# Start addresses of SBUF tiles in a two-layer encoder trunk, moved to multiples of 512 bytes

## Chip, core and metric

The kernel runs on one core of a Trainium2 chip. The metric is device time in microseconds (us) of one execution. A core has five engines with queues of their own: PE (TensorE, matrix products; its weight loads are shown apart as PEld), DVE (VectorE), ACT (ScalarE), POOL (GpSimd) and SP (SyncE, which here only issues DMA transfers). SBUF is the on-chip memory of 128 partitions that they work from; a tile is a range of bytes, the same in every partition. PSUM holds the results of PE.

## What is computed

Two layers of an encoder for one sequence of 512 tokens with 1024 features, everything in float32. Layer 0 mixes tokens with a state-space scan, layer 1 with a gated MLP; each is followed by a gated convolutional channel mixer, and every sub-layer by a layer norm.

```
for i in range(2):
    y = mamba2_mixer(x, ...) if i == 0 else spatial_gating_mixer(x, ...)
    x = layer_norm(DN_ALPHA * x + y, ln_g[i, 0], ln_b[i, 0])
    f = conv_ffn(x, ffn_w_in[i], ffn_conv_w[i], ffn_conv_b[i], ffn_w_out[i])
    x = layer_norm(DN_ALPHA * x + f, ln_g[i, 1], ln_b[i, 1])

def mamba2_mixer(x, ...):
    z, xbc, dt = split(x @ w_in)                 # 1024 -> 6176
    xbc = silu(causal_dwconv(xbc, conv_w, conv_b))
    y = ssd_scan(...) + d_skip * xs              # chunked state-space scan
    return rms_norm(y * silu(z), norm_g) @ w_out # 2048 -> 1024

def spatial_gating_mixer(x, ...):
    u, v = split(gelu(x @ w_in + b_in))          # 1024 -> 2 x 2048
    v = layer_norm(v, ln_g, ln_b)
    v = einsum('gts,bnsgc->bntgc', tril(w_s), v) + b_s
    return (u * v) @ w_out                       # 2048 -> 1024

def conv_ffn(x, ...):
    g, u = split(causal_dwconv(x @ w_in, conv_w, conv_b))  # 1024 -> 2 x 2816
    return (silu(g) * u) @ w_out                 # 2816 -> 1024
```

## The kernel before

Every large product is made from three PE products in the type float32r. Each operand is split into a rounded part `hi` and a rest `lo`, and `hi*hi + hi*lo + lo*hi` is added up in PSUM. All weights lie in one DRAM tensor of 244 pieces of 128 x 1024. `w_prep` brings each of them in: SP issues the load of `wraw` (3 buffers), ACT rounds it to `whi`, DVE subtracts to get `wlo` (7 buffers each), up to six pieces ahead of their use.

A matmul has a stationary operand, loaded into the array by a LDWEIGHTS of 128 columns of 4 bytes, and a moving operand that is streamed through it, here mostly 512 columns (2048 bytes in each partition). In this kernel every matmul has a weight load of its own. There are three kinds of products:

- Input projections (`mm_k`, lines 121 to 123, results `ip`): the weights `whi`/`wlo` are stationary, the activations `xT_hi`/`xT_lo` are moving. Eight of the tiles are done in two halves of 256 tokens (`InProj.pre` and `post`), so that PE has work while a layer norm ends.
- Output projections (`out_proj`, lines 211 to 213, results `acc`): the activations `ahi`/`alo` are stationary, the weights are moving. There are four: after the state-space scan (W_SO, 16 steps), after the first channel mixer (W_F1O, 22), after the gated MLP (W_GO, 16) and after the second channel mixer (W_F2O, 22).
- The v half of the gated MLP (`v_tile`, lines 560 to 562, results `pv`): `xT_hi`/`xT_lo` are stationary, the weights are moving. The first four tiles are started by `v_start`, while the layer norm before them ends; line 604 then adds the bias `bvb`, which ACT's queue loads at line 599 in four pieces (2 buffers).

What stands between them (scan, transposes, spatial product) uses plain float32 matmuls.

Tiles come from pools. `const` and `wpool` are laid out first and stay for the whole kernel; the other pools are opened and closed with the stages and take the space above, so a tile of one stage can lie on bytes that tiles of the stage before held, and its first writer then waits for their last reader. The allocator places every tile at the next multiple of 32 bytes. The order of each engine's instructions comes from a scheduler that follows the program's order and the waits. Some tiles are small: `nhalf` (16 numbers in a partition, the exponent of the reciprocal root on POOL), `ea`, `nsl`, `cd`, `rv` in the scan, and `st`, `mv`, `rs`, `vstat`, `vmv`, `vrs` of the layer norms. `ppt`, the table of per-channel constants, has 658 columns (2632 bytes).

Of the kernel before, what the change touches and what calls it, by code (L numbers as in the profile page):

```python
# [9 lines left out]
F32 = mybir.dt.float32  # L10
# [4 lines left out]
P = 128  # L15
T = 512
D = 1024
NT = T // P
# [26 lines left out]
C_ALL = C_LN + 64  # L45

KB = 4
WB = 7
LOOK = 6

# [2 lines left out]
def trunk_kernel(ctx, tc, x_tok, x_t, w_dt, wall, pp, ln_g, ln_b, b_v, b_s, w_s_t, out):  # L53
    nc = tc.nc

    const = ctx.enter_context(tc.tile_pool(name="const", bufs=1))
# [6 lines left out]

    def pool(stack, name, bufs=1):
        return stack.enter_context(tc.tile_pool(name=name, bufs=bufs, reuse_waits="tile"))

    wready = {}
    wnext = [0]
# [13 lines left out]
    def w_get(i, look=LOOK):  # L82
        w_prep(i + look)
        return wready.pop(i)

    xT_hi = const.tile([P, NK, T], F32R, name="xT_hi")
    xT_lo = const.tile([P, NK, T], F32R, name="xT_lo")
    xres = const.tile([P, NT, D], F32, name="xres")
    ppt = const.tile([P, C_ALL], F32, name="ppt")
    ident = const.tile([P, P], F32, name="ident")  # L90
    nhalf = const.tile([P, 16], F32, name="nhalf")
    ones = const.tile([P, P], F32, name="ones")

    def col(c):
        return ppt[:, c:c + 1]
# [106 lines left out]
    def out_proj(lnp, split, base, nk, ln, last, hooks=None, nxt=None, mid=None):  # L202
        if last:
            gb, bb = ln_bc(lnp, base, ln)
        acc = [[pst(f"acc{base}_{t}_{h}") for h in range(2)] for t in range(NT)]

        def mm(t, h, k, a, w):
            o = acc[t][h]
            ts_ = slice(t * P, (t + 1) * P)
            hs = slice(h * T, (h + 1) * T)  # L210
            nc.tensor.matmul(o, a[0][:, ts_], w[0][:, hs], start=(k == 0), stop=False)  # L211
            nc.tensor.matmul(o, a[0][:, ts_], w[1][:, hs], start=False, stop=False)  # L212
            nc.tensor.matmul(o, a[1][:, ts_], w[0][:, hs], start=False, stop=(k == nk - 1))  # L213

        k0 = 0
        if hooks is not None:
            k0 = 3
            aw = []
            for k in range(k0):
                aw.append((split.get(k), w_get(base + k, LOOK - k)))  # L220
                for t in range(NT - 1):
                    for h in range(2):
                        mm(t, h, k, *aw[k])
                hooks[0]() if k == 0 else None
            hooks[1]()
            for k in range(k0):
                for h in range(2):
                    mm(NT - 1, h, k, *aw[k])
            hooks[2]()
        nm = nk - (5 if last else KB)  # L230
        for k in range(k0, nm):
            a = split.get(k)
            w = w_get(base + k)
            for t in range(NT):
                for h in range(2):
                    mm(t, h, k, a, w)
            if k == 3 and mid is not None:
                mid()
        aw = []
        for k in range(nm, nk):  # L240
            aw.append((split.get(k), w_get(base + k, LOOK - (k - nm))))

        def tail(t):
            order = [(h, k) for h in range(2) for k in range(nm, nk)]
            if t == NT - 1 and not last:
                order = [(h, k) for k in range(nm, nk) for h in range(2)]
            for h, k in order:
                mm(t, h, k, *aw[k - nm])

        def stats(t):  # L250
            r = lnp.tile([P, D], F32, tag="r", bufs=2, name=f"r{base}_{t}")
            st = lnp.tile([P, 2, 6], F32, tag="st", bufs=2, name=f"st{base}_{t}")
            mv = lnp.tile([P, 2], F32, tag="mv", bufs=2, name=f"mv{base}_{t}")
            rs = lnp.tile([P, 2], F32, tag="rs", bufs=2, name=f"rs{base}_{t}")
            for h in range(2):
                hs = slice(h * T, (h + 1) * T)
                nc.vector.scalar_tensor_tensor(r[:, hs], xres[:, t, hs], ALPHA, acc[t][h], ALU.mult, ALU.add)
                nc.vector.bn_stats(st[:, h, :], r[:, hs])
            nc.vector.bn_aggr(mv, st)
            rstd_of(mv[:, 1:2], rs)  # L260
            for h in range(2):
                hs = slice(h * T, (h + 1) * T)
                if last:
                    nc.vector.scalar_tensor_tensor(
                        r[:, hs], r[:, hs], mv[:, 0:1], gb[:, hs], ALU.subtract, ALU.mult)
                    nc.vector.scalar_tensor_tensor(
                        r[:, hs], r[:, hs], rs[:, 1:2], bb[:, hs], ALU.mult, ALU.add)
                    nc.sync.dma_start(out[t * P:(t + 1) * P, hs], r[:, hs])
                else:
                    nc.vector.tensor_scalar(  # L270
                        xres[:, t, hs], r[:, hs], mv[:, 0:1], rs[:, 1:2], ALU.subtract, ALU.mult)

        def trans(t):
            for h in range(2):
                pt = pst(f"pt{base}_{t}_{h}")
                for q in range(4):
                    nc.tensor.transpose(  # L277
                        pt[:, q * P:(q + 1) * P], xres[:, t, h * T + q * P:h * T + (q + 1) * P], ident)
                xf = lnp.tile([P, 4, P], F32, tag="xf", bufs=2, name=f"xf{base}_{t}_{h}")
                for q in range(4):  # L280
                    c = C_LN + ln * 16 + 4 * h + q
                    nc.scalar.activation(  # L282
                        xf[:, q, :], pt[:, q * P:(q + 1) * P], AF.Identity, scale=col(c), bias=col(c + 8))
                xh = xT_hi[:, 4 * h:4 * h + 4, t * P:(t + 1) * P]
                nc.scalar.copy(xh, xf)
                nc.vector.tensor_sub(xT_lo[:, 4 * h:4 * h + 4, t * P:(t + 1) * P], xf, xh.bitcast(F32))

        for t in range(NT):
            tail(t)
            if t in (1, 2) and not last:  # L290
                trans(t - 1)
            with tc.high_priority():
                stats(t)
        if not last:
            nxt(trans)
# [22 lines left out]
            ip.post()  # L318
        return run

# [1 line left out]
    ip_f1 = InProj(W_F1I)  # L322
    with ExitStack() as st:
        yp = pool(st, "yp")
# [10 lines left out]
        ip = InProj(W_XBC)  # L335
        ip.ready[0] = ps_b0
        S, t4, s2, q, v, u = (xres[:, 3, i * P:(i + 1) * P] for i in range(6))
        ea = sc.tile([P, 1], F32, name="ea")
        nsl = sc.tile([P, 1], F32, name="nsl")
        nc.scalar.activation(v, ps_dt[:, 0:P], AF.Identity, bias=col(C_DT))  # L340
        nc.vector.scalar_tensor_tensor(u, v, -1.0, v, ALU.mult, ALU.min)
        nc.scalar.activation(u, u, AF.Exp)
# [29 lines left out]
        def ssd(g, cv):  # L372
# [2 lines left out]
            nc.sync.dma_start(R, bass.AP(  # L375
                tensor=scr.tensor, offset=scr.offset + 4 * g * T, ap=[[0, P], [T, 4], [1, T]]))
            EB = gp.tile([P, 2, 384], F32, tag="EB", bufs=1, name=f"EB{g}")
            cd = gp.tile([P, 4, NT], F32, tag="cd", bufs=2, name=f"cd{g}")
            pcb = pst(f"pcb{g}")
            for c in range(NT):  # L380
                cs = slice(c * P, (c + 1) * P)
# [99 lines left out]
        def rms(g, sq):  # L481
            pr = pst(f"pr{g}")
            nc.tensor.matmul(pr, ones, sq, start=True, stop=True)  # L483
            rt = zp.tile([P, 16, 32], F32, tag="rt", bufs=1, name=f"rt{g}")
            rv = zp.tile([P, 2, 16], F32, tag="rv", bufs=1, name=f"rv{g}")
            nc.vector.transpose(rt.rearrange("p a b -> p (a b)"), pr)
            nc.vector.tensor_scalar(rv[:, 0, :], rt[:, :, 0], 1.0 / 256.0, RMS_EPS, ALU.mult, ALU.add)
            nc.gpsimd.tensor_tensor(rv[:, 1, :], rv[:, 0, :], nhalf, ALU.pow)
            yield
            rb = zp.tile([P, T], F32, tag="rb", bufs=1, name=f"rb{g}")  # L490
            nc.vector.tensor_copy(rt, rv[:, 1, :].unsqueeze(2).broadcast_to([P, 16, 32]))
            nc.vector.transpose(rb, rt.rearrange("p a b -> p (a b)"))
            for k in range(2):
                yk = y[:, 2 * g + k, :]
                nc.vector.scalar_tensor_tensor(yk, yk, col(C_NG + 2 * g + k), rb, ALU.mult, ALU.mult)
# [28 lines left out]
                 hooks=[lambda: next(rg[6], None), lambda: next(rg[7]), lambda: next(rg[7], None)],  # L524
                 nxt=split_start(ip_f1))

# [1 line left out]
    def ffn(ip, base_o, li, ln, last, nxt=None):  # L528
        with ExitStack() as st:
            hp = pool(st, f"hp{li}")  # L530
# [19 lines left out]
            lnp = pool(st, f"lnp{li}")  # L550
            out_proj(lnp, split, base_o, 22, ln, last, nxt=nxt)

# [1 line left out]
    def v_tile(cb, t, ws):  # L554
        ps = pst(f"pv{cb}_{t}")
        ts_ = slice(t * P, (t + 1) * P)
# [20 lines left out]
    with ExitStack() as st:  # L577
# [4 lines left out]
        with ExitStack() as st2:  # L582
# [2 lines left out]
            wsr = vp.tile([P, 8, P], F32, name="wsr")  # L585
            rsb = vp.tile([P, 8, P], F32, name="rsb")
            bsb = vp.tile([P, 8, P], F32, name="bsb")
            vstat = vp.tile([P, NT, 4, 6], F32, name="vstat")
            nc.scalar.dma_start(wsr, w_s_t)
            nc.scalar.dma_start(bsb.rearrange("p g t -> p (g t)"), b_s.broadcast_to([P, D]))  # L590
            nc.gpsimd.affine_select(
# [2 lines left out]
            with ExitStack() as st3:  # L594
                vq = pool(st3, "vq")
                for cb in range(4):
# [5 lines left out]
                    for t in range(NT):  # L602
# [2 lines left out]
                        nc.scalar.activation(v2[:, t, cs], v2[:, t, cs], AF.Gelu_apprx_tanh)  # L605
                        nc.vector.bn_stats(vstat[:, t, cb, :], v2[:, t, cs])
                        if cb == 3:
                            mv = vq.tile([P, 2], F32, tag="vmv", bufs=2, name=f"vmv{t}")
                            rs = vq.tile([P, 2], F32, tag="vrs", bufs=2, name=f"vrs{t}")
                            nc.vector.bn_aggr(mv, vstat[:, t])  # L610
                            rstd_of(mv[:, 1:2], rs)
                            nc.vector.tensor_scalar(
# [132 lines left out]
```

## Time and profile before

| | |
|---|---|
| time, median of 3 runs | 1477.07 us (1477.03 to 1477.26) |
| profiled execution, first to last instruction (span) | 1475.1 us |
| median of the runs less that span | 1.97 us |
| PE busy | 1461.5 us, 6911 matmuls |
| PEld busy | 1189.7 us |
| DVE, ACT, POOL busy | 859.3, 609.0, 41.1 us |

The profile is of one execution, and gives its span; what lies around the span is taken from the difference to the median of the runs. A matmul's own duration in the profile includes its way through the array and overlaps with its neighbours', so how fast matmuls follow each other is read from the distance between their starts.

### The profile page before, as it was taken

The page shows a single profiled execution, that of the slowest core. Times are in us where ns is not written, and L with a number is a line of the kernel's source. Part 1 is how long each engine was busy: PE and PEld are TensorE (multiplying, and loading weights), DVE is VectorE, ACT ScalarE, POOL GpSimd, SP SyncE. Part 2 cuts the span into 40 slices and gives each one's busy share as a digit, 9 for nine tenths or more (in the row PEclk, how much of TensorE's full clock was granted, in tenths as well). Part 3 has the DMA queues.
Part 4 walks back from the last instruction along what each step waited for, and adds up shares of the span by engine and source line. Part 5 has one row for each costly group of instructions (what it writes and reads, how often), then busy time and mean ns, then how long its engine had stood idle before and what let it go on. Part 6 is the DMA issues. An engine that isn't in the chain of part 4 may idle for free.

```text
span 1475.1 us, 17344 instructions
## 1 busy us (share of the span) xinstructions
PE 1461.5 (99%) x6911; PEld 1189.7 (81%) x6911; DVE 859.3 (58%) x1171; ACT 609.0 (41%) x893; POOL 41.1 (3%) x36
## 2 busy tenths in 40 slices
PE   8999999999999999999999999999999999999997
PEld 5888778777889888888888887888888888888886
DVE  6778777665557755555335646447367655554336
ACT  4786577433335433333223533223245433333220
POOL 0000000122000000000000000000000000000001
PEclk9999999999999999999999999999999999999999
DMA  6634321421313423333231423223323333324211
GB/s 207 207 100 129 101 100 59 142 86 58 115 57 111 143 90 100 87 98 107 94 100 58 149 99 109 73 86 115 98 65 125 114 90 97 100 86 128 97 46 57
DMA packets 42560, 150.55 MB, mean 102 GB/s; under 512 B 4720, under 2 KB 6000, under 8 KB 41456
## 3 DMA queue, kind: packets, MB, share of 16 engines
q1 hardware_dynamic: 39792, 140.93, 30.5%
q10 hardware_dynamic: 2688, 8.52, 1.8%
q8 instruction: 54, 0.88, 0.2%
q14 instruction: 26, 0.21, 0.0%
HBM read 147.27 MB, written 2.16 MB: 101 GB/s over the span
## 4 chain that ended last, share of the span: by engine, by line
PE 99%; DMA 0%; DVE 0%; issue 0%; SPq 0%; ACT 0%; DVEq 0%
PE ip L123 19%; PE ip L121 19%; PE ip L122 19%; PE acc L211 9%; PE acc L212 9%; PE acc L213 9%; PE pv L560 2%; PE pv L561 2%; PE pv L562 2%; PE py L442 1%; PE psp L620 1%; PE pst L427 1%; PE po L451 1%; PE pt L277 1%; PE pcb L382 0%; PE pr L483 0%
## 5 line engine op out<-in xcount | busy, mean ns | idle before, releaser
L121 PE MATMUL ip<-xT_hi,whi 128*128 128x512 f32 (+1 forms) x1264 | 490.4, 388 | 0.0
L123 PE MATMUL ip<-xT_hi,wlo 128*128 128x512 f32 (+1 forms) x1264 | 487.2, 386 | 0.0
L122 PE MATMUL ip<-xT_lo,whi 128*128 128x512 f32 (+1 forms) x1264 | 484.2, 383 | 0.0
L78 DVE TENSOR_TENSOR wlo<-wraw,whi 128x1024 fp32r<-128x1024 f32 x242 | 295.5, 1223 | 289.4 <-ACT whi L76 288.7
L76 ACT CAST whi<-wraw 128x1024 fp32r<-128x1024 f32 x242 | 253.2, 1049 | 365.6 <-PE ip L122 296.3
L122 PEld LDWEIGHTS ip<-xT_lo,whi 128*128 128x128 f32 x1264 | 237.7, 188 | 53.0 <-issue 1.7
L121 PEld LDWEIGHTS ip<-xT_hi,whi 128*128 128x128 f32 x1264 | 237.4, 188 | 53.1 <-issue 2.0
L123 PEld LDWEIGHTS ip<-xT_hi,wlo 128*128 128x128 f32 x1264 | 237.2, 188 | 50.5
L211 PE MATMUL acc<-whi,ahi 128*128 128x512 f32 x608 | 238.3, 392 | 0.0
L212 PE MATMUL acc<-wlo,ahi 128*128 128x512 f32 x608 | 237.1, 390 | 0.0
L213 PE MATMUL acc<-whi,alo 128*128 128x512 f32 x608 | 236.7, 389 | 0.0
L211 PEld LDWEIGHTS acc<-whi,ahi 128*128 128x128 f32 x608 | 114.2, 188 | 24.5 <-issue 0.5
L213 PEld LDWEIGHTS acc<-whi,alo 128*128 128x128 f32 x608 | 114.1, 188 | 24.3
L212 PEld LDWEIGHTS acc<-wlo,ahi 128*128 128x128 f32 x608 | 114.2, 188 | 23.9 <-issue 0.5
L190 DVE TENSOR_TENSOR alo<-h,ahi 128x512 fp32r<-128x512 f32 x44 | 30.4, 690 | 101.5 <-ACT ahi L189 101.5
L189 ACT CAST ahi<-h 128x512 fp32r<-128x512 f32 x44 | 27.4, 623 | 140.6 <-PE acc L212 115.6
L177 DVE SCALAR_TENSOR_TENSOR cv<-ip,ppt,cv 128x511 f32<-128x511 f32 (+2 forms) x93 | 69.2, 744 | 3.5 <-ACT cv L175 2.3
L177 DVE SCALAR_TENSOR_TENSOR ut<-ip,ppt,ut 128x511 f32<-128x511 f32 x88 | 65.7, 746 | 1.8 <-ACT ut L175 0.5
L177 DVE SCALAR_TENSOR_TENSOR gt<-ip,ppt,gt 128x511 f32<-128x511 f32 x88 | 65.6, 746 | 1.3
L547 ACT ACTIVATE gt<-gt 128x512 f32<-128x512 f32 x44 | 27.8, 632 | 84.4 <-DVE gt L177 84.3
L282 ACT ACTIVATE xf<-pt,ppt 128x128 f32<-128x128 f32 x96 | 36.6, 467 | 46.2 <-PE pt L277 44.1
L560 PE MATMUL pv<-whi,xT_hi 128*128 128x512 f32 x128 | 50.9, 398 | 0.0
(144 smaller groups left out, 1118.8 us busy)
## 6 DMA issues: line engine op xcount, KB each, us to landing
wraw<-in_wall_dram SPq DMA_DIRECT2D x242, 512.0 KB, 3.6
xres<-scr SPq DMA_DIRECT2D x8, 1024.0 KB, 4.8
xr<-in_x_t_dram SPq DMA_DIRECT2D x8, 256.0 KB, 5.0
xres<-in_x_tok_dram ACTq DMA_DIRECT2D x1, 2048.0 KB, 7.7
out_dram<-r SPq DMA_DIRECT2D x8, 256.0 KB, 2.0
wraw_s<-in_wall_dram SPq DMA_DIRECT2D x8, 128.0 KB, 4.7
lngf<-in_ln_g_dram ACTq DMA_DIRECT2D x2, 512.0 KB, 4.0
lnbf<-in_ln_b_dram ACTq DMA_DIRECT2D x2, 512.0 KB, 4.9
```

The source lines that it names most:

```text
L76: nc.scalar.copy(hi, raw)
L78: nc.vector.tensor_sub(lo, raw, hi.bitcast(F32))
L121: nc.tensor.matmul(o, whi[:, cs], xT_hi[:, k, lo:hi], start=(k == 0), stop=False)
L122: nc.tensor.matmul(o, whi[:, cs], xT_lo[:, k, lo:hi], start=False, stop=False)
L123: nc.tensor.matmul(o, wlo[:, cs], xT_hi[:, k, lo:hi], start=False, stop=(k == NK - 1))
L177: nc.vector.scalar_tensor_tensor(o[:, s:], ps[:, :T - s], col(c + taps - 1 - s), o[:, s:], ALU.mult, ALU.add)
L190: nc.vector.tensor_sub(lo, self.act(k), hi.bitcast(F32))
L211: nc.tensor.matmul(o, a[0][:, ts_], w[0][:, hs], start=(k == 0), stop=False)
L212: nc.tensor.matmul(o, a[0][:, ts_], w[1][:, hs], start=False, stop=False)
L213: nc.tensor.matmul(o, a[1][:, ts_], w[0][:, hs], start=False, stop=(k == nk - 1))
L282: nc.scalar.activation(xf[:, q, :], pt[:, q * P:(q + 1) * P], AF.Identity, scale=col(c), bias=col(c + 8))
L560: nc.tensor.matmul(ps, xT_hi[:, k, ts_], whi, start=(k == 0), stop=False)
```

## The change

The small tiles of `const` and of the scan become slices of one tile `small` of 96 columns, which stands first; `ppt` is moved behind the other tiles of `const` and is rounded up to 768 columns; and the small tiles of the layer norms are each rounded up to 128 columns. Everything else keeps its size. The first tile after `small` then begins at a multiple of 512 bytes, and so do all that follow. The diff without the removed comments:

```
+HEAD = 96
...
+    def block(pl, n, name, tag=None, bufs=1):
+        return pl.tile([P, -(-n // P) * P], F32, tag=tag or name, bufs=bufs, name=name)[:, 0:n]
...
+    small = const.tile([P, HEAD], F32, name="small")
+    nhalf = small[:, 0:16]
     xT_hi = const.tile([P, NK, T], F32R, name="xT_hi")
     xT_lo = const.tile([P, NK, T], F32R, name="xT_lo")
     xres = const.tile([P, NT, D], F32, name="xres")
-    ppt = const.tile([P, C_ALL], F32, name="ppt")
     ident = const.tile([P, P], F32, name="ident")
-    nhalf = const.tile([P, 16], F32, name="nhalf")
     ones = const.tile([P, P], F32, name="ones")
+    ppt = block(const, C_ALL, "ppt")
...
-            st = lnp.tile([P, 2, 6], F32, tag="st", bufs=2, name=f"st{base}_{t}")
-            mv = lnp.tile([P, 2], F32, tag="mv", bufs=2, name=f"mv{base}_{t}")
-            rs = lnp.tile([P, 2], F32, tag="rs", bufs=2, name=f"rs{base}_{t}")
+            st = block(lnp, 12, f"st{base}_{t}", "st", 2).rearrange("p (a b) -> p a b", a=2)
+            mv = block(lnp, 2, f"mv{base}_{t}", "mv", 2)
+            rs = block(lnp, 2, f"rs{base}_{t}", "rs", 2)
...
-        ea = sc.tile([P, 1], F32, name="ea")
-        nsl = sc.tile([P, 1], F32, name="nsl")
+        ea = small[:, 16:17]
+        nsl = small[:, 17:18]
...
-            cd = gp.tile([P, 4, NT], F32, tag="cd", bufs=2, name=f"cd{g}")
+            cd = small[:, 32 + 16 * (g % 2):48 + 16 * (g % 2)].rearrange("p (h c) -> p h c", h=4)
...
-            rv = zp.tile([P, 2, 16], F32, tag="rv", bufs=1, name=f"rv{g}")
+            rv = small[:, 64:96].rearrange("p (a b) -> p a b", a=2)
...
-            vstat = vp.tile([P, NT, 4, 6], F32, name="vstat")
+            vstat = block(vp, NT * 24, "vstat").rearrange("p (t c s) -> p t c s", t=NT, c=4)
...
-                            mv = vq.tile([P, 2], F32, tag="vmv", bufs=2, name=f"vmv{t}")
-                            rs = vq.tile([P, 2], F32, tag="vrs", bufs=2, name=f"vrs{t}")
+                            mv = block(vq, 2, f"vmv{t}", "vmv", 2)
+                            rs = block(vq, 2, f"vrs{t}", "vrs", 2)
```

Where the operands of the float32r matmuls begin, as the rest of the byte address in the partition after division by 512, in the two built programs. Each operand is a slice at a multiple of 512 bytes within its tile, so this is the rest of every operand. The difference in the last column is that of the two starts, weights less moving, again as a rest of 512.

| product | matmuls | moving, before | weights, before | difference before | both, after |
|---|---|---|---|---|---|
| input projections, 512 columns | 3456 | 128 | 288 | 160 | 0 |
| input projections, 256 columns | 384 | 128 | 288 | 160 | 0 |
| v half of the gated MLP | 384 | 288 | 128 | 352 | 0 |
| output projection after the scan | 384 | 288 | 480 | 192 | 0 |
| the other three output projections | 1440 | 288 | 288 | 0 | 0 |

On PE and SP the instructions stand in the same order as before. On ACT, DVE and POOL a few stand elsewhere, because tiles now lie on other bytes and wait for other readers. The place that matters below is the loading of the bias `bvb` (bytes 221344 to 225439 before, 222208 to 226303 after). Before, the first two pieces stood on ACT in the last steps of the first channel mixer (names carry buffer numbers; `gt`, `ut` and `h` are tiles of the channel mixer):

```order
L175 ACTIVATE gt_21_5199<-ip_5201,ppt 128x512 [waits PE_49]
L547 ACTIVATE gt_21_5199<-gt_21_5199 128x512 [waits DVE_49,Activation_49]
L76 CAST whi_5293<-wraw_5291 128x1024 [waits DMAHW1_49,PE_49]
L175 ACTIVATE ut_21_5200<-ip_5232,ppt 128x512 [waits PE_49]
L599 DMA bvb_6309<-in_b_v_dram 128x512
L599 DMA bvb_6323<-in_b_v_dram 128x512
L76 CAST whi_5323<-wraw_5321 128x1024 [waits DMAHW2_49,PE_49]
L189 CAST ahi_6_5487<-h_3774 128x512
```

They stand now behind the last transposes of the layer norm that follows (`xf` is a tile of that layer norm, `wsr` and `bsb` are other tables of the gated MLP):

```order
L287 ACTIVATE xf_3_1_6210<-pt_3_1_6205,ppt 128x128 x3
L290 CAST xT_hi<-xf_3_1_6210 128x4x128 [waits Activation_49]
L594 DMA wsr<-in_w_s_t_dram 128x1024
L595 DMA bsb<-in_b_s_dram 128x1024 [waits DVE_49,Pool_49]
L604 DMA bvb_6291<-in_b_v_dram 128x512 [waits DVE_49]
L604 DMA bvb_6305<-in_b_v_dram 128x512
L80 CAST whi_6309<-wraw_6307 128x1024 [waits DMAHW0_49,PE_49]
L80 CAST whi_6315<-wraw_6313 128x1024 [waits DMAHW1_49,PE_49]
L610 ACT_TABLE_LOAD
```

The two loads were free of waits and are now issued when DVE has read `xf` for the last time. On DVE, the four additions of the bias and the weight piece that the next v tile needs stood so before (`v` is the result, `pv` the v tiles):

```order
L604 TENSOR_TENSOR v_6298<-pv_0_6137,bvb_6309 128x512 [waits PE_49]
L604 TENSOR_TENSOR v_6298<-pv_1_6186,bvb_6309 128x512 [waits PE_49]
L604 TENSOR_TENSOR v_6298<-pv_2_6235,bvb_6309 128x512 [waits PE_49]
L606 BN_STATS vstat<-v_6298 128x6 [waits Activation_49] x3
L604 TENSOR_TENSOR v_6298<-pv_3_6260,bvb_6309 128x512 [waits PE_49]
L78 TENSOR_TENSOR wlo_6329<-wraw_6325,whi_6327 128x1024 [waits DMAHW2_49,Activation_49]
```

and stand so now:

```order
L609 TENSOR_TENSOR v_6280<-pv_0_6119,bvb_6291 128x512 [waits DMAHW5_49,PE_49]
L609 TENSOR_TENSOR v_6280<-pv_1_6168,bvb_6291 128x512 [waits PE_49]
L609 TENSOR_TENSOR v_6280<-pv_2_6217,bvb_6291 128x512 [waits PE_49]
L609 TENSOR_TENSOR v_6280<-pv_3_6242,bvb_6291 128x512 [waits PE_49]
L82 TENSOR_TENSOR wlo_6311<-wraw_6307,whi_6309 128x1024 [waits DMAHW0_49,Activation_49]
L611 BN_STATS vstat<-v_6280 128x6 [waits Activation_49] x4
```

The first addition also waits for the transfer now, and the weight piece is queued behind it.

## Rows read from the trace of the kernel before

**Rows 1.** The page: span, busy times, granted TensorE clock, chain that ended last.
```profile
span 1475.1 us, 17344 instructions
...
PE 1461.5 (99%) x6911; PEld 1189.7 (81%) x6911; DVE 859.3 (58%) x1171; ACT 609.0 (41%) x893; POOL 41.1 (3%) x36
...
PEclk9999999999999999999999999999999999999999
...
PE 99%; DMA 0%; DVE 0%; issue 0%; SPq 0%; ACT 0%; DVEq 0%
```

**Rows 2.** Groups by line and shape: count, busy us, mean ns, idle before.
```profile
L121 PE MATMUL ip<-xT_hi,whi 128*128 128x512 f32 x1136 | 454.0, 400 | 0.0
...
L122 PEld LDWEIGHTS ip<-xT_lo,whi 128*128 128x128 f32 x1264 | 237.7, 188 | 53.0 <-issue 1.7
...
L211 PE MATMUL acc<-whi,ahi 128*128 128x512 f32 x608 | 238.3, 392 | 0.0
...
L560 PE MATMUL pv<-whi,xT_hi 128*128 128x512 f32 x128 | 50.9, 398 | 0.0
...
L121 PE MATMUL ip<-xT_hi,whi 128*128 128x256 f32 x128 | 36.4, 285 | 0.0
```

**Rows 3.** Timeline of PE, input projection, 512 columns: start us, us.
```profile
500.17 0.39 PE L121 MATMUL ip<-xT_hi,whi 128*128 128x512 f32 x1
...
504.37 0.39 PE L121 MATMUL ip<-xT_hi,whi 128*128 128x512 f32 x1
```

**Rows 4.** Timeline of PE, output projection after the gated MLP.
```profile
1061.82 0.39 PE L211 MATMUL acc<-whi,ahi 128*128 128x512 f32 x1
...
1065.90 0.39 PE L211 MATMUL acc<-whi,ahi 128*128 128x512 f32 x1
```

**Rows 5.** Timeline of PE, output projection after the scan.
```profile
382.23 0.39 PE L211 MATMUL acc<-whi,ahi 128*128 128x512 f32 x1
...
387.73 0.39 PE L211 MATMUL acc<-whi,ahi 128*128 128x512 f32 x1
```

**Rows 6.** Timeline of PE, v half of the gated MLP.
```profile
860.24 0.40 PE L560 MATMUL pv<-whi,xT_hi 128*128 128x512 f32 x1
...
865.86 0.40 PE L560 MATMUL pv<-whi,xT_hi 128*128 128x512 f32 x1
```

**Rows 7.** Timeline of PE, input projection in halves of 256 columns.
```profile
441.70 0.28 PE L121 MATMUL ip<-xT_hi,whi 128*128 128x256 f32 x1
...
443.13 0.28 PE L121 MATMUL ip<-xT_hi,whi 128*128 128x256 f32 x1
```

**Rows 8.** Timelines of ACT's DMA issues at the two places of the bias.
```profile
690.77 0.82 ACTq L599 DMA_DIRECT2D bvb<-in_b_v_dram  x2
...
829.74 0.33 ACTq L590 DMA_DIRECT2D bsb<-in_b_s_dram  x1
```

**Rows 9.** Timeline of DVE, start of the gated MLP.
```profile
828.96 0.69 DVE L286 TENSOR_TENSOR xT_lo<-xf,xT_hi 128x512 fp32r<-128x512 f32 x1 [1.01 <-ACT xT_hi L285]
829.57 2.04 DVE L604 TENSOR_TENSOR v<-pv,bvb 128x512 f32<-128x512 f32 x3
...
836.54 0.69 DVE L604 TENSOR_TENSOR v<-pv,bvb 128x512 f32<-128x512 f32 x1 [2.60 <-PE pv L562]
837.15 1.22 DVE L78 TENSOR_TENSOR wlo<-wraw,whi 128x1024 fp32r<-128x1024 f32 x1
```

**Rows 10.** DMA issues: count, KB each, median us from issue to landing.
```profile
bvb<-in_b_v_dram ACTq DMA_DIRECT2D x4, 256.0 KB, 3.7
...
bsb<-in_b_s_dram ACTq DMA_DIRECT2D x1, 512.0 KB, 4.2
```

**Rows 11.** Busy us (and count) of each engine in the first 40 us; clock; DMA.
```profile
0.00:40.00 40.00, 34.38 (x173) 22.62 (x174) 26.66 (x53) 20.44 (x33) 0.95 (x7) 1.00 0.63 211
```

## Prediction

> **What bounds the kernel now.** I read the page first, then the groups by shape, then the timeline of PE in each kind of product. The page [rows 1] shows PE busy for 1461.5 of 1475.1 us and on 99% of the chain that ended last, with the granted clock in the top tenth in all 40 slices (the 2.4 GHz level). The groups of matmuls have no idle time before them [rows 2]. So the end moves only with the distance at which PE starts one matmul after another, or with a new wait for PE. DVE and ACT, busy for 58% and 41%, have room.
>
> That distance isn't the same everywhere, though all these matmuls have 128 rows, 128 weight columns and the same type, and those of 512 columns are alike in shape:
>
> - input projections: 18 steps from 500.17 to 504.37 us, 4.20 us, 233.3 ns each [rows 3];
> - output projection after the gated MLP: 18 steps, 4.08 us, 226.7 ns [rows 4]; the two after the channel mixers have the same starts and run the same code;
> - output projection after the scan: 24 steps, 5.50 us, 229.2 ns [rows 5];
> - v half of the gated MLP: 24 steps, 5.62 us, 234.2 ns [rows 6];
> - input projections of 256 columns: 12 steps, 1.43 us, 119.2 ns [rows 7].
>
> As a check: 3456 x 233.3 + 1440 x 226.7 + 384 x (229.2 + 234.2 + 119.2) ns is 1356 us; the remaining 105 us of PE's busy time are the plain float32 matmuls.
>
> Now lay the table of starts beside this. The weights begin at rest 288 both in the input projections (233.3) and in the later output projections (226.7), so the weights' start alone doesn't sort the distances. The moving operand begins at rest 288 both in the v half (234.2) and in the later output projections (226.7), so its start alone doesn't either. The difference of the two does: 0 gives 226.7, 192 gives 229.2, 160 gives 233.3, 352 gives 234.2. The cleanest pair is rows 4 against rows 5: the same three lines of code, the same loops, the same moving tiles, and only the weights' rest differs, 288 against 480, with 2.5 ns between them. My reading is that the weight load of the next matmul and the moving stream of the present one disturb each other in SBUF by their relative position, least when both begin at the same rest. The weight loads (188 ns each [rows 2]) do run beside the streaming.
>
> One rule speaks against this reading. The Trainium skill (TensorE: Matmul & The Clock Gate, Step-by-step: what each phase is for) says that PE has two independent SBUF read ports and that loading the next weights takes no read bandwidth from the running matmul. Rows 4 and 5 disagree with it by 2.5 ns a matmul; by the rule the sum below would be nothing, by the rows it is 26 us. It is kept as a rival.
>
> **The change part by part.** After the change every pair has the difference 0, with both starts at rest 0. No row shows rest 0; the nearest is the one with the same difference, 226.7 ns, and I take it. Bounds: 234.2 ns, the slowest row, on one side; on the other, one clock period of 2.4 GHz for each column, 213.3 ns.
>
> - Input projections of 512 columns: 3456 less the 48 of the first two tiles, which go at the pace of the first loads, are 3408 (3 lines of 1136 [rows 2]). 3408 x (233.3 - 226.7) = 22.5 us less.
> - v half: 3 x 128 = 384 matmuls [rows 2], 384 x (234.2 - 226.7) = 2.9 us less.
> - Output projection after the scan: 16 steps x 24 = 384, 384 x (229.2 - 226.7) = 1.0 us less.
> - The other three output projections: 3 x 608 less those 384 are 1440, unchanged, 0.
> - Input projections of 256 columns, 384. No row shows them with the difference 0. They take 119.2 ns, 12.5 over one period for each column (106.7), while the best 512-column row is 13.4 over its 213.3; so what is left over looks like a part that every matmul has, and I take 0. Bounds: 0, and the same share as the long ones, 2.8% of 119.2 or 3.4 ns, 1.3 us less.
> - Plain float32 matmuls: some 105 us. Their starts change too, but no row here sorts them by it. I take 0; bounds plus and minus 1 us, 1% of them.
> - The first 40 us: PE is busy for 34.38 of 40.00 [rows 11], waiting for the first loads. If these land sooner in tiles on even starts, up to 1 us is gained; I take 0. Transfers later are hidden behind PE.
> - The slices of `small` and the rounded tiles change no instruction's size. Sharing one tile could make DVE, POOL and ACT wait for each other in the scan; POOL is busy 41.1 us in all and PE waits for none of it [rows 1]. 0.
> - The bias loads are moved. They were issued at 690.77 us, 139 us before their use; now they go out when DVE has read `xf`, at 829.65 (828.96 + 0.69), behind `bsb`, which was issued at 829.74 and takes 4.2 us, to 833.9 [rows 8, 9, 10]. A bias piece takes 3.7 us from its issue at about 830.1, to 833.8; if it must wait for `bsb` to end and then needs the time for its half as many bytes, some 1.5 us, it is 835.4. Three additions stood at 829.57 [rows 9]; now all four run from 833.8 or 835.4 for 4 x 0.69 us, and the weight piece `wlo` (1.22) behind them ends between 837.8 and 839.4. It was done at 838.37. PE needs it for the seventh of eight steps of the next v tile, 18 matmuls after that tile's start at about 836.5 (the fourth v tile ended when DVE could go on, 836.54), that is at 840.7, or 840.0 with the faster matmuls of this tile and the three before it. The banks that the following v tiles write into were those of the transposes, free already. So the move is hidden, with 0.6 us to spare; if that cover fails, each us by which the bias lands later is one us of PE, and I bound this at 2 us.
>
> Sum: 22.5 + 2.9 + 1.0 = 26.4 us less. Against the profiled execution that is a span of 1475.1 - 26.4 = 1448.7 us; the median of the runs lies 1.97 us over the span, so the time is **1450.7 us**, 1.8% less. The small bounds together (1.3 + 1 + 1 gained, 1 + 2 lost) make 1447 to 1454 of this case.
>
> **Rivals.**
> *More than that.* Equal rests are good, and rest 0 is better still. For it speaks only that no row has rest 0. At its bound of 213.3 ns it gives 3408 x 20.0 + 384 x 20.9 + 384 x 15.9 + 1440 x 13.4 + 384 x 12.5 ns = 106 us less, 1371 us. Against it speaks the 12 to 13 ns that short and long matmuls alike have over one period for each column. The Trainium skill (TensorE: Matmul & The Clock Gate, Back-to-back issue gap) gives N/2.4 + 2.5 ns, 215.8 ns for 512 columns; by that the estimate would be about 1384 us. No row here comes nearer than 226.7.
>
> *No change.* The distances come from something else that goes with the kinds of product: the results' banks, which change every 3 matmuls in output projections and every 24 elsewhere, or the work that DVE and ACT do beside. This is also what the rule of the two ports gives. Against it speaks the pair of rows 4 and 5, which share all that. Time 1477.
>
> *Slower.* An even start is itself the bad case: two operands that both begin at a multiple of 512 ask for the same part of the memory at the same moment, and every pair of 512 columns goes at the slowest row, 234.2. Then 1440 x 7.5 + 384 x 5.0 + 3408 x 0.9 ns = 15.8 us are added, 1493 us. It decides from the point where the distance at rest 0 is over 231.4 ns: the 5616 matmuls of 512 columns in the sum take 1299 us now. Against it: an equal rest of 288 is the best row there is.
>
> *The new wait bites.* The bias lands several us late and PE waits for `wlo`, here or in the tiles after: 2 to 13 us on top of the forecast, 1453 to 1464 us.
>
> **How the numbers follow.** The forecast has 0.68, more than that 0.13, no change 0.10, slower 0.06, the new wait 0.03. The predicted time is that of the forecast. The range goes up to 1464, which takes in the new wait, and down to 1400, which takes in about 0.08 of the 0.13 if it is spread evenly from 1371 to 1444: together 0.79. A measurement of this kernel can tell about 0.2%, 3 us. Faster than that: 0.68 + 0.13 + 0.03 = 0.84; within it 0.10; slower 0.06.
>
> **What would show it.** In the profile after, three matmuls of an input projection should start over 0.68 us instead of 0.70, and the v half and the output projection after the scan should go at the same 226.7 ns, with the later output projections unchanged. If these too get faster, even starts count and not only equal ones; if rows 3 and 6 stand, the starts aren't the cause. A wait of PE for `wlo` or of DVE for `bvb` near 815 to 825 us would show the moved loads. The prediction is wrong if the distance at rest 0 isn't that of equal rests at 288.

## The result and the profile after

The changed kernel takes 1453.09 us (median; 1451.56 to 1454.75, 4 runs) against 1477.05 (1476.84 to 1477.26, 4 runs) before on the same chip: a ratio of 0.9836 with a 95% interval of 0.9822 to 0.985. It is 24.0 us, 1.6%, faster. 1450.7 was forecast.

The page of the profile after, the lines that answer to [rows 1]:

```profile
span 1449.8 us, 17347 instructions
...
PE 1436.0 (99%) x6911; PEld 1188.8 (82%) x6911; DVE 859.3 (59%) x1171; ACT 610.2 (42%) x893; POOL 41.2 (3%) x36
...
PEclk9999999999999999999999999999999999999999
...
PE 96%; DMA 1%; DVE 1%; ACT 1%; issue 0%; SPq 0%; DVEq 0%
```

PE has the same 6911 matmuls at the same granted clock, and is busy for 25.5 us less (1461.5 - 1436.0); the span is 25.3 us shorter. DVE is busy as before, POOL to 0.1 us and ACT to 1.2 us. So the gain lies in the distance at which matmuls follow each other. The timelines of PE after, for the five stretches of [rows 3 to 7] (start us, own us), each from the first to the last of a gapless piece. First an input projection, 18 steps:

```profile
489.83 0.39 PE L126 MATMUL ip<-xT_hi,whi 128*128 128x512 f32 x1
...
493.91 0.39 PE L126 MATMUL ip<-xT_hi,whi 128*128 128x512 f32 x1
```

The output projection after the scan, 24 steps:

```profile
374.69 0.39 PE L216 MATMUL acc<-whi,ahi 128*128 128x512 f32 x1
...
380.13 0.39 PE L216 MATMUL acc<-whi,ahi 128*128 128x512 f32 x1
```

The v half of the gated MLP, 24 steps:

```profile
845.03 0.39 PE L565 MATMUL pv<-whi,xT_hi 128*128 128x512 f32 x1
...
850.47 0.39 PE L565 MATMUL pv<-whi,xT_hi 128*128 128x512 f32 x1
```

The output projection after the gated MLP, 18 steps:

```profile
1042.85 0.39 PE L216 MATMUL acc<-whi,ahi 128*128 128x512 f32 x1
...
1046.93 0.39 PE L216 MATMUL acc<-whi,ahi 128*128 128x512 f32 x1
```

An input projection in halves of 256 columns, 12 steps:

```profile
434.97 0.28 PE L126 MATMUL ip<-xT_hi,whi 128*128 128x256 f32 x1
...
436.40 0.28 PE L126 MATMUL ip<-xT_hi,whi 128*128 128x256 f32 x1
```

| distance of starts, ns | difference before | before | difference after | after |
|---|---|---|---|---|
| input projection, 512 columns | 160 | 233.3 [rows 3] | 0 | 226.7 |
| v half | 352 | 234.2 [rows 6] | 0 | 226.7 |
| output projection after the scan | 192 | 229.2 [rows 5] | 0 | 226.7 |
| output projection after the gated MLP | 0 | 226.7 [rows 4] | 0 | 226.7 |
| input projection, 256 columns | 160 | 119.2 [rows 7] | 0 | 119.2 |

The difference is that of the prediction: where the stationary operand of a matmul begins, less where its moving operand begins, in bytes modulo 512. (The stationary operand is a weight piece in the input projections; in the v half and the output projections it is the activations, and the weight piece is moving.) Three kinds of product have come down to the distance that the fourth had already, and the two that were forecast to stay have stayed.

How the gain grows along the program was read by setting the start of each matmul before against that of the same matmul after. It is 6.7 us by the end of the output projection after the scan, 13.1 behind the first channel mixer, 18.3 behind the gated MLP and 24.7 at the last matmul. It comes with the 512-column matmuls whose difference has changed; over the output projections that had 0 before it stands still (13.06 to 13.11 us and 18.26 to 18.30 us over the first two of them). The last 0.5 us lie behind the last matmul, where the stores are issued as soon as before; they come in the closing instructions of the program. All the traces of kernels built on the changed one have them (7.8 to 7.9 us from the start of the last matmul to the end), the two with the old layout don't (8.3 and 8.4). Why isn't known.

### The profile page after: what moved, and what is told of

Read it like the earlier page. It is cut to its first block, busy times and chain, and to the rows that moved or that the text cites. A ratio compares the mean times of both kernels' runs of the same rounds, so it can differ in the third digit from the quotient of the medians.

```text
span 1449.8 us, 17347 instructions
## 1 busy us (share of the span) xinstructions
PE 1436.0 (99%) x6911; PEld 1188.8 (82%) x6911; DVE 859.3 (59%) x1171; ACT 610.2 (42%) x893; POOL 41.2 (3%) x36
## 4 chain that ended last, share of the span: by engine, by line
PE 96%; DMA 1%; DVE 1%; ACT 1%; issue 0%; SPq 0%; DVEq 0%
PE ip L126 18%; PE ip L127 18%; PE ip L128 18%; PE acc L218 10%; PE acc L216 10%; PE acc L217 10%; PE pv L567 2%; PE pv L566 2%; PE pv L565 2%; PE py L447 1%; PE psp L625 1%; PE pst L432 1%; PE po L456 1%; PE pt L282 1%; DMA xres<-scr 1%; PE pr L488 0%
## 5 line engine op out<-in xcount | busy, mean ns | idle before, releaser
L127 PE MATMUL ip<-xT_lo,whi 128*128 128x512 f32 (+1 forms) x1264 | 478.7, 379 | 0.0
L128 PE MATMUL ip<-xT_hi,wlo 128*128 128x512 f32 (+1 forms) x1264 | 478.5, 379 | 0.0
```

What stands on the lines that cost most here:

```text
L127: nc.tensor.matmul(o, whi[:, cs], xT_lo[:, k, lo:hi], start=False, stop=False)
L128: nc.tensor.matmul(o, wlo[:, cs], xT_hi[:, k, lo:hi], start=False, stop=(k == NK - 1))
```

## The experiments

The theory was: the difference of the two starts sets the distance, and nothing else in the change matters. The rivals were: that an even start is good in itself; that the distances go with the kinds of product and not with the starts; and that the moved bias loads or the rounded small tiles are part of the account. "Mean distance" below is the mean time from the start of one matmul to that of the next of the same kind, without the few distances over 250 ns, where another instruction or a wait stands between.

**The changed kernel again.** No edit, on the chip of the next experiments.

> The changed kernel once more, beside the others on the same chip. It gave 1451.56, 1452.07, 1454.75 and 1454.12 us in four runs, a spread of 3.2 us where the kernel before has 0.4. If the spread lies in the first group of the scan, where PE now waits for the decay factors, a profile of a longer run has more idle time of PE between 40 and 80 us and the same distances elsewhere; the median stays at 1451 to 1455.

1452.07 us (1450.73 to 1453.73) against 1478.09 (1476.96 to 1480.64): ratio 0.9821, 0.9808 to 0.9835. The runs of the kernel before spread over 3.7 us on this chip too, so the spread of 3 us after isn't made by the change. The profile is of one of its shorter executions (1451.73 us); the one at rest 256 below is of a longer one, and where its time goes is told further down.

**Every tile at rest 32.** The changed kernel with a head that is one step of 32 bytes longer: no tile begins evenly, every difference stays 0.

```
-HEAD = 96
+HEAD = 104
```

> The changed kernel with 32 bytes more in its first tile, so that every tile begins at rest 32 of 512 and no difference between starts is touched. If the difference between the two operands' starts is what counts, the distances stay at 226.7 ns and the time at that of the changed kernel, within 3 us. If it is the even start itself, the distances go back to 231 to 234 ns and the time to 1470 to 1480 us.

1452.17 us, ratio 0.9823 (0.981 to 0.9837). The timeline of PE in an input projection of this run:

```profile
489.69 0.39 PE L126 MATMUL ip<-xT_hi,whi 128*128 128x512 f32 x1
...
493.77 0.39 PE L126 MATMUL ip<-xT_hi,whi 128*128 128x512 f32 x1
```

18 steps in 4.08 us: 226.7 ns, and means of 226.8 to 227.1 in all three kinds. Multiples of 512, which the change was made for, are not needed.

**Only `xT` moved.** The kernel before, with two lines moved so that `xT_hi` and `xT_lo` begin at rest 288 like the weights. The small tiles, the bias loads and the later pools stay as before; the output projection after the scan keeps its difference of 192.

```
     ones = const.tile([P, P], F32, name="ones")
+    xT_hi = const.tile([P, NK, T], F32R, name="xT_hi")
+    xT_lo = const.tile([P, NK, T], F32R, name="xT_lo")
```

> The kernel before with one edit: xT_hi and xT_lo are allocated last in their pool, so that they begin at rest 288 as the weights do; every other tile above stays on its bytes, the output projection after the scan keeps its difference of 192, and the bias loads stay where they were. If the difference of the starts is the cause, the input projections and the v half go at 226.7 ns at an uneven start, and of the 26.4 us 25.4 are gained: 1451.7 us by that sum, some 1.7 us more if the changed kernel's shortfall at its start is met here too. If even starts are the cause, 1477 us.

1453.04 us, ratio 0.983 (0.9816 to 0.9843). Its input projection:

```profile
490.10 0.39 PE L121 MATMUL ip<-xT_hi,whi 128*128 128x512 f32 x1
...
494.18 0.39 PE L121 MATMUL ip<-xT_hi,whi 128*128 128x512 f32 x1
```

Again 226.7 ns; the output projection after the scan has a mean of 229.0 still, the others and the v half 226.8. The order of two allocations gives nearly the whole gain. The kinds of product are the same as before, so they aren't what set 233.3.

**Only the weights moved off.** The changed kernel with a table of another width ahead of the weights: the weights and all later pools begin at rest 160, `xT` at 0. That gives back the differences of before (160 and 352), with 0 in all output projections, and keeps everything else of the change.

```
-    ppt = block(const, C_ALL, "ppt")
+    ppt = const.tile([P, 680], F32, name="ppt")[:, 0:C_ALL]
```

> The changed kernel with one edit: the table ahead of the weights is 680 columns long instead of 768, so that the weights and everything above begin at rest 160 and xT_hi, xT_lo at 0. The differences of 160 and 352 are those of the kernel before for the input projections and the v half, at other absolute rests; all output projections have the difference 0. If the difference counts, 3408 x 6.6 ns and 384 x 7.5 ns come back, 25.4 us: 1475 to 1479 us. If absolute starts count, it can lie anywhere else, and stays near 1453 us if starts have nothing to do with it.

1476.2 us, ratio 0.9996 (0.9987 to 1.0005): no faster than before. Its input projection:

```profile
489.76 0.39 PE L126 MATMUL ip<-xT_hi,whi 128*128 128x512 f32 x1
...
493.96 0.39 PE L126 MATMUL ip<-xT_hi,whi 128*128 128x512 f32 x1
```

18 steps take 4.20 us again, 233.3 ns, the distance of [rows 3]. One number takes the whole gain back, and the output projections stay at 226.8 to 226.9. With the run before, this shows the difference as the cause in both directions.

**Without the small layer-norm tiles.** The changed kernel with `st`, `mv`, `rs`, `vstat`, `vmv` and `vrs` at their old sizes. The operands still begin at 0, and the bias loads are back at their old place.

```
-            st = block(lnp, 12, f"st{base}_{t}", "st", 2).rearrange("p (a b) -> p a b", a=2)
+            st = lnp.tile([P, 2, 6], F32, tag="st", bufs=2, name=f"st{base}_{t}")
...
-            vstat = block(vp, NT * 24, "vstat").rearrange("p (t c s) -> p t c s", t=NT, c=4)
+            vstat = vp.tile([P, NT, 4, 6], F32, name="vstat")
```

> The changed kernel with the small tiles of the layer norms at their old sizes. All operands of the float32r matmuls still begin at rest 0, and the bias loads stand where they stood in the kernel before, free of waits. If the moved loads are hidden, the time is that of the changed kernel within 1 us (1451 to 1454); if PE waits for them, it is 2 us or more shorter.

1452.66 us, ratio 0.9832 (0.9818 to 0.9847). The timeline of DVE of this run at the bias, and then the one of the changed kernel:

```profile
815.87 1.90 DVE L609 TENSOR_TENSOR v<-pv,bvb 128x512 f32<-128x512 f32 x3
...
822.52 0.69 DVE L609 TENSOR_TENSOR v<-pv,bvb 128x512 f32<-128x512 f32 x1 [2.27 <-PE pv L567]
823.12 1.22 DVE L82 TENSOR_TENSOR wlo<-wraw,whi 128x1024 fp32r<-128x1024 f32 x1
```

```profile
820.77 2.71 DVE L609 TENSOR_TENSOR v<-pv,bvb 128x512 f32<-128x512 f32 x4 [4.54 <-DMA bvb<-in_b_v_dram]
823.40 1.21 DVE L82 TENSOR_TENSOR wlo<-wraw,whi 128x1024 fp32r<-128x1024 f32 x1
```

The moved loads do make DVE wait for 4.54 us, but the weight piece behind them ends at 824.61 and not at 824.34, 0.3 us later. The time doesn't tell the two kernels apart.

**Maps of the difference.** Three runs, of one execution each, put the seven buffers of the weights at seven different rests in one run.

The first gave each buffer of both halves 1032 columns, so that `whi` and `wlo` of one piece had different rests:

```
-            hi = wpool.tile([P, 1024], F32R, tag="whi", bufs=WB, name=f"whi{i}")
+            hi = wpool.tile([P, 1032], F32R, tag="whi", bufs=WB, name=f"whi{i}")[:, 0:1024]
```

> The changed kernel with a pitch of 4128 instead of 4096 bytes between the seven buffers of whi and of wlo, so that these begin at rests 0, 32, ... 192 and 224, ... 416, while xT_hi and xT_lo stay at 0 and the stationary parts of the output projections go to 448. One trace then holds differences of the two starts from 0 to 480 in steps of 32. If the difference counts, the distance of the input projections is 226.7 ns where the next weights begin at 0, and near 233 where they begin at 160, as before; the output projections get slower than 226.7 wherever the difference isn't 0, near 229 at 192. If only evenness of either start counts, there are two levels, one for rest 0 and one for the others. The time lies between 1453 and 1490 us in both cases.

It took 1478.58 us and didn't sort: the pieces with `whi` at difference 0 and `wlo` at 224 went at 231.0 on the mean, not 226.7 for two matmuls of three, and all groups lay between 229.6 and 233.4. A badly placed operand slows the matmuls next to it as well. As a map it is inconclusive.

The other two therefore gave both halves of one piece the same rest, one from 0 to 192 and one from 224 to 416:

```
-            hi = wpool.tile([P, 1024], F32R, tag="whi", bufs=WB, name=f"whi{i}")
+            hi = wpool.tile([P, 1024], F32R, tag=f"whi{i % WB}", name=f"whi{i}")
...
-            lo = wpool.tile([P, 1024], F32R, tag="wlo", bufs=WB, name=f"wlo{i}")
+            lo = wpool.tile([P, 1032], F32R, tag=f"wlo{i % WB}", name=f"wlo{i}")[:, 0:1024]
```

and in the second of them `ppt` has 696 columns.

> In the map before, whi and wlo had different rests, and no matmul had a neighbour of the same kind; there even a difference of 0 gave 231 ns. Here each of the seven pairs of whi and wlo begins at one common rest, 0, 32, ... 192, with xT_hi and xT_lo at 0 and the stationary parts of the output projections at 224. So each weight piece is 24 matmuls with one difference: 0 to 192 in the input projections, 224 to 32 in the output projections. If the difference counts by itself, the input projections go at 226.7 ns at 0 and at 233.3 at 160, the output projections at 229.0 at 192, as before at those differences, whatever the absolute rests. If a mixture of weights is what slows, the distances don't sort by the difference. Time between 1460 and 1480 us.

> The same with all weights 224 bytes further: differences 224 to 416 in the input projections; in the output projections again 224 to 32, at other absolute rests. If only the difference counts, the output projections repeat the distances of the run before to 0.5 ns at each difference; if absolute rests matter too, they don't. Whether 256 is as good as 0 shows how far apart two starts may be and still count as equal. Time between 1460 and 1480 us.

They took 1480.23 and 1482.86 us, a little above the expected 1460 to 1480: in each, one buffer in seven has a difference of 0 or 256, and the output projections lose what they had. The distances in ns, as means of threes (a third of the time from the first matmul with `whi` to the next such), for the input projections of the channel mixers and of the u half over both runs (some 100 threes each), and for the output projections in the first and in the second run (some 80 each, the same differences at other rests):

| difference, bytes | 0 | 32 | 64 | 96 | 128 | 160 | 192 | 224 |
|---|---|---|---|---|---|---|---|---|
| input projections | 228.0 | 233.0 | 233.4 | 233.8 | 233.3 | 233.5 | 229.4 | 233.4 |
| the same, plus 256 | 228.1 | 233.0 | 233.4 | 233.8 | 233.1 | 233.3 | - | - |
| output projections, first run | - | 233.1 | 233.4 | 233.7 | 233.3 | 233.4 | 229.9 | 233.0 |
| output projections, second run | - | 233.1 | 233.3 | 233.7 | 233.1 | 233.4 | 229.9 | 233.0 |

The columns repeat within 0.2 ns after 256 bytes where both were run (192 and 224 plus 256 weren't), and within 0.2 ns when both operands are moved. There are two good values in 256 bytes, 0 and 192. The 1.3 to 1.4 ns over 226.7 at differences 0 and 256 lie at the ends of such a piece: its first nine matmuls are slower, most of all the first (235 ns), and so is the last (235), behind which the next piece comes; those between go at 226.6 to 226.7.

The two maps show something more for the halves of 256 columns, where the changed kernel has a steady 120.0 ns. The timeline of PE in a half tile at difference 64, in the first of them:

```profile
457.94 0.28 PE L127 MATMUL ip<-xT_hi,whi 128*128 128x256 f32 x1
...
459.98 0.28 PE L127 MATMUL ip<-xT_hi,whi 128*128 128x256 f32 x1
```

18 steps in 2.04 us are 113.3 ns. So matmuls of 256 columns depend on the starts too, and 0 isn't their best difference. Of the four half tiles at 320 in the second map, one goes at 113.5 and three at 117 to 118, so the difference doesn't settle their distance by itself.

**The weights at rest 256.** The changed kernel with `ppt` at 704 columns: half of the modulus that the change works with.

```
-    ppt = block(const, C_ALL, "ppt")
+    ppt = const.tile([P, 704], F32, name="ppt")[:, 0:C_ALL]
```

> The changed kernel with the table ahead of the weights 704 columns long, so that the weights and everything above begin at rest 256 of 512 and xT_hi, xT_lo at 0: differences of 256 in the input projections and the v half, 0 in the output projections. The two maps read as if differences repeat every 256 bytes (288 like 32, 320 like 64, 416 like 160), so all distances should be 226.7 ns and the time that of the changed kernel, 1450 to 1455 us. If only 512 counts as equal and the map's 228 ns at 256 was a mixture, the input projections are at 228 ns or more and the time at 1457 us or above.

1452.25 us, ratio 0.9827 (0.9813 to 0.984). Its input projection:

```profile
489.72 0.39 PE L126 MATMUL ip<-xT_hi,whi 128*128 128x512 f32 x1
...
493.80 0.39 PE L126 MATMUL ip<-xT_hi,whi 128*128 128x512 f32 x1
```

226.7 ns with the weights 256 bytes off: 256 counts as equal for matmuls of 512 columns.

## Why the prediction was right

**The mechanism** held, as far as it says that the difference of the starts counts and not the rest itself: that is shown by the runs at rest 32 and 288 (as fast) and at 160 (gain gone). The step "I take the row with the same difference, 226.7 ns" held to a tenth of a nanosecond in all gapless pieces.

**The terms.** They were sized from gapless pieces. The last column goes by the two traces, matmul by matmul: by how much sooner the next one starts after than before.

| term | forecast, us | mean distances, ns | measured, us |
|---|---|---|---|
| input projections, 512 columns, 3408 | 22.5 | 233.36 to 227.06 | 21.2 |
| v half, 384 | 2.9 | 234.27 to 226.80 | 2.8 |
| output projection after the scan, 384 | 1.0 | 228.98 to 227.01 | 0.8 |
| other output projections | 0 | 226.83 to 226.74 | 0.1 |
| input projections, 256 columns | 0 | 119.9 to 119.8 | -0.1 |
| float32 matmuls, without the wait below | 0 | - | 0.1 |
| start, up to the 61st matmul | 0 | - | 0.4 |
| a new wait in the scan | 0 | - | -0.6 |

Together 24.7 us at the last matmul, and 25.2 with the closing, against 26.4 forecast. The miss is in the first term, over-sized by a twentieth. After the change, the second to the tenth matmul of an input projection behind each of 56 changes from another kind of product go at 227.3 to 232.7 ns on the mean, and 226.7 holds from the eleventh on; before, they are hardly slower than the rest (233.5). That is 1.3 us in all, and the pieces that the term was sized from stand clear of such places. The float32 matmuls were taken at 0 within 1 us; they gave 0.1. That the forecast time, 1450.7 us, lies 2.4 under the median has a second part: the profiled execution took 1451.56 us, the shortest of the four (see the start, below).

The 0 for 256 columns came out, but its reason did not. If 12 to 13 ns over one period for each column were "a part that every matmul has", nothing could be gained there, and the first map has a half tile at 113.3 ns, 6.6 over the 106.7. So the 0 was right for these two differences by luck.

The waits of PE in the profile after:

```profile
PE ps_dt L119 <- DMA wdt<-in_w_dt_dram: 5.1, 1, 5.1
PE ps_dt L119 <- DMA xr<-in_x_t_dram: 1.0, 1, 1.0
PE pst L432 <- ACT btok L412: 0.2, 1, 0.2
```

**The start.** The first load took 5.1 us, 4.6 before, which is scatter (4.1 in the second profile of the same kernel). PE is ahead of before all the same when it comes to its 61st matmul, at 15.43 us for 15.79. Its first matmuls are slow up to some point and quick from there on, and the point moves from execution to execution. Two rows of the timeline of PE after, and two of the run at rest 256, whose profile is of its longest execution (1453.51 us):

```profile
10.29 0.63 PE L126 MATMUL ps_b<-xT_hi,whi_s 128*128 128x512 f32 x1
...
11.74 0.39 PE L128 MATMUL ps_b<-xT_hi,wlo_s 128*128 128x512 f32 x1
```

```profile
16.74 0.63 PE L128 MATMUL ps_b<-xT_hi,wlo_s 128*128 128x512 f32 x1
...
18.05 0.39 PE L127 MATMUL ps_b<-xT_lo,whi_s 128*128 128x512 f32 x1
```

The traces' own entries of the granted clock begin at 11.4 and 17.5 us, at the full 2.4 GHz level. A clock that is lower until then would look like this, but no entry shows it (the 1.00 in [rows 11] has none behind it for the first 13 us). In the five profiles of kernels whose 512-column matmuls all have a difference of 0 or 256, the 61st matmul starts at 15.4 (twice), 15.7, 17.1 and 17.7 us, and what follows takes 1433.8 to 1434.6. So the 2.2 us by which these five spans differ lie in the start, and not in the first group of the scan, where they were expected.

**The new wait.** The third row of the waits is new. The timeline of PE shows it in the scan's first group:

```profile
60.26 0.39 PE L128 MATMUL ip<-xT_hi,wlo 128*128 128x512 f32 x1
...
60.80 1.13 PE L432 MATMUL pst<-xw,btok 128*128 128x256 f32 x4 [0.15 <-ACT btok L412]
```

From 60.26 to 60.80 are 0.54 us where 0.23 is usual: 0.3 us lost, and another 0.3 in two smaller gaps of the same group. PE comes to this place 1.3 us earlier than before, and ACT's `btok` only 0.75 (60.27 for 61.02). The chain that ended last names what ACT was behind with there:

```profile
43.46 8.45 DMA xres<-scr
52.16 4.68 ACT E L404 x16
57.58 1.80 ACT E L407
```

A load of 8.45 us, then the 16 activations and the exponential of the first group. The second profile of the changed kernel has the same wait, 0.4 us; the one at rest 32, with the same code, doesn't, and there PE comes 1.7 us later from the start. The forecast has no term for it: it looked for new waits at the bias and among the engines that share `small`. A faster PE made a place with little cover into a wait.

**The moved loads** were hidden, as forecast. The first addition came 4.55 us after DVE was free (its `xT_lo` at 815.53 takes 0.69, the addition starts at 820.77), within the forecast 4.2 to 5.8, and `wlo` was done at 824.61. The fourth v tile ends near 822.5 (DVE's row at 822.52 in the run without the moved loads), and 18 matmuls of 226.7 ns later, at about 826.6, PE wanted the piece: some 2 us to spare instead of 0.6, because the bias landed at the early one of the two times. PE's v tiles run through without a gap; its timeline after:

```profile
819.19 0.39 PE L565 MATMUL pv<-whi,xT_hi 128*128 128x512 f32 x1
...
831.43 0.39 PE L565 MATMUL pv<-whi,xT_hi 128*128 128x512 f32 x1
```

54 steps in 12.24 us, 226.7 ns.

**The rivals.** "More than that" fell: rest 0 gives 226.7 ns like rests 32 and 288. "No change" fell with the run that moved only `xT`, and "slower" with the same distances at rest 0. What the Trainium skill (TensorE: Matmul & The Clock Gate, Step-by-step: what each phase is for) says of the two independent ports, that loading the next weights takes no read bandwidth from the running matmul, would give no difference between these kernels. By itself it does not fit the pair of 1452 and 1476 us from one number in an allocation; whether it is the two reads that meet, no row shows.

**What stays open.** The runs show that the relative position of the two operands decides. That the load of the next weights and the present stream collide in SBUF is the prediction's reading; no row shows a collision, and a kernel without weight loads of its own for each matmul was not tried. Why 192 is better than its neighbours isn't known either, nor what sorts the distances of 256 columns, nor why the quick matmuls set in at another time in each execution. The runs over 1453.6 us have no profile, so that their time also goes into the start is not shown.

## What to carry to other kernels

Where PE bounds a kernel and each matmul loads weights of its own, measure the distance between starts for each kind of product: two values for one shape and type are a reason to print the SBUF addresses of both operands. In this kernel those of 512 moving columns should begin at equal places modulo 256 bytes; absolute alignment brought nothing, and rounding up the small layer-norm tiles, which PE doesn't read, brought nothing that the times show. An odd-sized table ahead of a pool shifts everything behind it: here 24 us hung on the width of one.

## What was not expected of the hardware

- For 512 columns the pattern repeats every 256 bytes and not 512, and has a second good value: 229.4 to 229.9 ns at a difference of 192, against 233.0 to 233.8 at every other multiple of 32 except 0.
- Matmuls of 256 columns go by another pattern: means of 119.9 ns at a difference of 160 and 119.8 at 0, but 113.3 in a half tile at 64.
- A badly placed operand slows its neighbours: in the first map, two of three matmuls had difference 0 and the three went at 231.0 ns on the mean. Behind a change from another kind of product it takes some ten matmuls until 226.7 holds.
- 226.7 ns for 512 columns is the lowest mean distance of a kind of product in any run here, 13.4 over one period of 2.4 GHz for each column, at whatever equal rest.
